# A decoder block on one core: where the small products stand among the dense ones, from the first columns to the attention

## The chip, the cores and the metric

One Trainium2 chip, one of its cores. The time is that of one execution on the device in microseconds (us). TensorE (PE in the profile) does matrix products, VectorE (DVE), ScalarE (ACT) and GpSimd (POOL) work element by element, SyncE (SP) issues most DMAs. Each engine takes its instructions in the order in which the program lists them; across engines they wait on semaphores.

## What is computed

A hybrid decoder block for 1024 tokens of 1024 channels: attention over low-rank latents (8 heads) and an RWKV-7 recurrence (8 heads of 64), merged by sigmoid gates, then a feed-forward and a gated embedding.

```python
h = rmsnorm(x, g_mix)
z_mla, z_rwkv, z_gate = split(h @ w_in)            # 672, 1792 and 2048 columns
# recurrence: token shift of z_rwkv, then r, k, v (512 columns each) and three low-rank inputs
decay = exp(-exp(-softplus(-(w0 + tanh(w_lo) @ w2)) - 0.5)); a = sigmoid(a0 + a_lo @ a2); g = sigmoid(g_lo) @ g2
kk = k * k_k / norm(k * k_k)
S_t = S_{t-1} diag(decay_t) + (S_{t-1} a_t) b_t^T + v_t k_t^T ;  y_t = S_t r_t     # 1024 steps
y_b = (groupnorm(y) + bonus) * g @ w_o_rwkv
# attention: q and k, v from normed latents, rotary tables of 32 dimensions, causal softmax
y_a = attention(rmsnorm(c_q) @ w_uq, rmsnorm(c_kv) @ w_ukv, rope(k_pe)) @ w_o_mla
x = x + (sigmoid(gate_a) * y_a + sigmoid(gate_b) * y_b) @ w_out
x = x + relu(h2 @ w_ffn_up)**2 @ w_ffn_down ;  x = x + sigmoid(h3 @ w_ple_gate) * (p @ w_ple_proj) ;  rmsnorm(x)
```

## The kernel before

The columns of `h @ w_in` are made 128 at a time by `dense`: the weights are split into a high and a low part (`wh` by ACT, `wl` by DVE), and 48 products of 128x128 by 128x512 (`psd<-xh,wh`, `psd<-xl,wh`, `psd<-xh,wl`; 8 blocks, 3 terms, 2 halves) fill one accumulator, which ACT and DVE then evacuate. 16 such units are the columns of the gates (`gate_units`); nothing reads them before the merge after the attention, so the kernel uses them as filler.

The generators yield an estimate of the work they have traced, and `weave` traces the stream that is furthest behind its share. That decides the order on each engine. The stages are:

- **First columns** (52 to 142 us): the columns of the low-rank inputs (`evac_lo`), two of the four key columns (`evac_k`; two came earlier), then 12 low-rank accumulators (`lora`: decay, a and g), the norm of the keys (`n`, `sn`, `rn`, `rns`: ACT and DVE on 8 rows), the first two r columns (`evac_rv`), and the products `nb`, which spread the norm over the channels for `kz`.
- **Early stage** (142 to 367 us): the stream `main` (columns of the latents, the rest of r, v, then gate units) is woven with `early(g)` for 8 groups of 128 tokens and with two triangular inverses. `inverse` has a long DVE part (`prd`, `X`), a way through DRAM (`xt_d`, `mt`), two transposes on DVE (`x0`), and then small products of 32x32 (`y<-x,lr` and `y<-mt,y2s`, called y products below). The second inverse is the last of the stage.
- **Recurrence** (367 to 575 us): per group `pre(g+1)` loads and prepares the next group, `chain` does two chunks of 64 tokens (products `pc`, solve, `py`, `vT`, the new state W), `finish` normalises (`yT`, `yn`, `yh`, `yl`). Gate units go between them, in half columns (`pg`). `T_LATE` and `T_MAIN` set the shares. `T_LEFT = 60` (in the scheduler's own units) is kept back.
- **Preparation** (575 to 644 us): the last `finish`, and then the attention's latents (`latf`, split into `chi` and `clo`), rotary tables (`posi`, `tab`, `kpr`), value weights, first values and queries, woven with the gates kept back (`T_REST`).
- **Attention, merge, feed-forward, embedding** (from 644 us).

`tc.issue_after(ins)` puts the instructions that are traced inside it behind `ins` on their own engine. In `together` the first product of a bundle may move up, and the rest stand behind it:

```python
first = mms[0]()
with tc.issue_after(first.ins):
    for f in mms[1:]:
        last = f()
```

Of the kernel before, what the change touches and what calls it, by code (L numbers as in the profile page):

```python
# [11 lines left out]
F32 = mybir.dt.float32  # L12
# [57 lines left out]
def tile_block(  # L70
# [147 lines left out]

    def mm_steps(acc, wh, wl, kb, rh, rl):

        for wt, rr in ((wh, (rh, rl)), (wl, (rh,))):
            for k in range(kb):
                for ri, r in enumerate(rr):
                    for h in range(2):
                        T.matmul(acc[:, h, :], lhsT=wt[:, k, :], rhs=r[k][:, h * 512:h * 512 + 512],  # L225
                                 start=wt is wh and k == 0 and ri == 0, stop=wt is wl and k == kb - 1)
                yield 0.43 * len(rr)
# [30 lines left out]
    def run(g):  # L258
        for _ in g:
            pass  # L260
# [5 lines left out]
    def lazy(f):  # L266
        yield from f()

# [86 lines left out]
    with s0:  # L355
# [91 lines left out]
        run(dense(w_in, 0, NB, MLA_COLS + RD + 2 * P, 2 * P, xh, xl, evac_k, m0=2))  # L447
# [8 lines left out]
        for which in range(3):  # L456
            for j in range(4):
                cs = slice(j * P, (j + 1) * P)
                acc = psd(s="lora")
                terms = [(wt, t) for wt in (lw_h, lw_l) for t in lora_in[which]]  # L460
                if which == 2:
                    terms.pop()
                for h in range(2):
                    hs = slice(h * 512, h * 512 + 512)
                    for i, (wt, t) in enumerate(terms):
                        T.matmul(acc[:, h, :], lhsT=wt[:, which, cs], rhs=t[:, hs], start=i == 0, stop=i == len(terms) - 1)
                t = ta("sa")
                if which < 2:
                    A.activation(t, flat(acc), AF.Sigmoid, bias=pcol(("w0", "a0")[which], j))
                    nc.sync.dma_start(sa_d[which, cs, :], t)  # L470
                else:
                    A.copy(t, flat(acc))
                    nc.sync.dma_start(g_d[cs, :], t)
# [23 lines left out]
        run(dense(w_in, 0, NB, MLA_COLS, RV0 * P, xh, xl, evac_rv))  # L497

        for j in range(4):
            acc = psd(s="nb")  # L500
            for h in range(2):
                T.matmul(acc[:, h, :], lhsT=selt[0:32 + H, j, :], rhs=rns[0:32 + H, h * 512:h * 512 + 512], start=True, stop=True)
            V.scalar_tensor_tensor(kz[j], kz[j], pcol("k_k", j), flat(acc), ALU.mult, ALU.mult)
            nc.sync.dma_start(kh_d[j * P:(j + 1) * P, :], kz[j])

    p0.close()

    with ExitStack() as wk:
# [32 lines left out]
        def norm_latent(ms, n, g, i):  # L541
            rb = te("rb")
            sumsq_rstd(src["early"], sqt[ms[0] >= 3], n, rb, i)
# [24 lines left out]
        def until(g, cost):  # L568

            done = 0.0  # L570
            while done < cost:
                c = next(g, None)
                if c is None:
                    return
                done += c
                yield c

        def latent_cols():
            q = dense(w_in, 0, NB, 0, QR, xh, xl, evac_c)
            yield from dense(w_in, 0, NB, QR, KVR, xh, xl, evac_c, m0=3)  # L580
            yield from until(q, 12)
            yield from norm_latent((3, 4), KVR, "g_kv", 0)
            yield from q
            yield from kpe_raw()
            yield from norm_latent((0, 1, 2), QR, "g_q", 1)
# [3 lines left out]
            dense(w_in, 0, NB, MLA_COLS + RV0 * P, RD - RV0 * P, xh, xl, evac_rv, m0=RV0),  # L589
# [3 lines left out]
        def gate_units():  # L593

            for m in range(2 * NB):
                raw = load_w(w_in, 0, NB, G0 + m * P, P)
                wh, wl = split_w([(lambda t: t, raw)], NB, P)
                if "half" not in psq:
                    acc = psd()
                    yield from mm_steps(acc, wh, wl, NB, xh, xl)  # L600
                    evac_gate(m, acc)
                    continue
                t = src["gt"]()
                for h in range(2):
                    hs = slice(h * 512, h * 512 + 512)
                    acc = psq["p"].tile([P, 512], F32, tag="pg", bufs=2, name=nm("pg")) if "half" in psq else psd()[:, 0, :]
                    for wt, rr in ((wh, (xh, xl)), (wl, (xh,))):
                        for k in range(NB):
                            for ri, r in enumerate(rr):
                                T.matmul(acc, lhsT=wt[:, k, :], rhs=r[k][:, hs], start=wt is wh and k == 0 and ri == 0, stop=wt is wl and k == NB - 1)  # L610
# [36 lines left out]
        with ExitStack() as rg:  # L647
            ep = src["early"] = pool(rg, "early")

            def early(g):  # L650
# [14 lines left out]
                for c in range(2):  # L665
                    ps = psa((P, 4, CH), s="L")
                    for j in range(4):
                        for h in range(2):
                            R = LOH[h]
                            T.matmul(ps[R, j, :], lhsT=c8(a)[R, 2 * j + c, :], rhs=c8(ah)[R, 2 * j + c, :], start=True, stop=True)  # L670
# [5 lines left out]
            def inverse(b):  # L676
# [31 lines left out]
                yield 3  # L708
                for c in range(8):
                    y2 = psa((P, 4, CH), s="y2")  # L710
                    for j in range(4):
                        for h in range(2):
                            Rt, Rb = slice(h * 64, h * 64 + 32), slice(h * 64 + 32, h * 64 + 64)
                            T.matmul(y2[Rb, j, 0:32], lhsT=lr[Rt, c * 4 + j, :], rhs=x0[Rt, c * 4 + j, :], start=True, stop=True)
# [22 lines left out]
        with ExitStack() as rg:  # L737
            kp = pool(rg, "late")

            def pre(g):  # L740
# [37 lines left out]
                for c in range(2):  # L778
                    ar = kp.tile([P, 8, CH], F32, tag="ar", bufs=4, name=nm("ar"))
                    scs = psx.tile([P, 2, 4, P], F32, tag="sc", bufs=1, name=nm("sc"))  # L780
                    for j in range(4):
                        for h in range(2):
                            R = LOH[h]
                            T.matmul(scs[:, h, j, :], lhsT=sh[R, 2 * j + c].rearrange("q b t -> q (b t)"),
                                     rhs=q3[R, h:3:2 - h, 2 * j + c, :], start=True, stop=True)
# [27 lines left out]
            def chain(ci):  # L813
# [37 lines left out]
                yield 1  # L851
# [19 lines left out]
                yield 1  # L871
# [52 lines left out]
    with ExitStack() as rg:  # L924
# [12 lines left out]
        def rope_tables():  # L937
# [22 lines left out]
            t, kpr = slot(12, F32, "kpt"), slot(16, F32, "kpr")  # L960
# [15 lines left out]
        with ExitStack() as pst:  # L976
# [82 lines left out]
            prep = chainit(latents(), lazy(rope_tables), value_weights(), values(0, V0, psa_v), queries(0, psv))  # L1059
# [686 lines left out]
```

## Time and profile before

| what | value |
|---|---|
| median of 3 runs | 1776.8 us (1774.46 to 1779.6) |
| profiled execution | 1779.02 us, of which 1777.3 us from its first to its last instruction |
| mean granted TensorE clock | 0.984 |
| PE busy | 1700.4 us (96% of the span) |
| DVE, ACT, POOL busy | 1199.6, 834.2 and 259.4 us |

A wait row names the engine and tile that waited, the engine and tile that ended the wait, the total, the number of times and the longest. A timeline row has the start, the length, engine, line, operation, tiles and count, and in brackets the idle time of that engine just before. The chain of waits goes back from the last instruction over what released each one.

### The profile page before, as it was taken

To read this page: it belongs to the slowest core of one execution; us is meant where nothing else is said; L and a number is where in the kernel's file an instruction comes from. 1 tells how busy PE (TensorE), PEld (TensorE's weight loads), DVE (VectorE), ACT (ScalarE), POOL (GpSimd) and SP (SyncE) were. 2 spreads that over 40 slices of the span, in tenths; PEclk is the share of its full clock that TensorE was granted. 3 is DMA by queue.
4 is the path that set the end of the run, shared out by engine and by line. 5 is a ranking of instruction groups with operands and counts; after the bars stand their busy time and mean duration, and the time that the engine had idled before them with its cause. 6 is when DMAs were issued, how large, how long until landed. Compare 5 with 4: busy or idle time off the path is not lost.

```text
span 1777.3 us, 26927 instructions
## 1 busy us (share of the span) xinstructions
PE 1700.4 (96%) x10525; PEld 1382.4 (78%) x10525; DVE 1199.6 (67%) x1882; ACT 834.2 (47%) x1418; POOL 259.4 (15%) x206
## 2 busy tenths in 40 slices
PE   7999999799999989998999999999999999999997
PEld 6877877677777867776888877888888888888886
DVE  6546695857777578887264368555568787687655
ACT  5553424244443366665344156555566344354444
POOL 2000000000000022121000203333332333332000
PEclk9999999989999999999999999999999999999999
DMA  6257765645553510015353324535557755451402
GB/s 196 72 204 217 202 199 128 183 102 140 159 141 96 168 44 25 25 60 190 107 153 108 110 116 143 166 131 159 167 182 249 238 167 160 148 178 48 154 12 96
DMA packets 245695, 246.14 MB, mean 138 GB/s; under 512 B 48729, under 2 KB 194752, under 8 KB 245568
## 3 DMA queue, kind: packets, MB, share of 16 engines
q1 hardware_dynamic: 243792, 239.65, 43.8%
q0 software_dynamic: 1760, 4.76, 0.8%
q8 instruction: 83, 1.36, 0.3%
q14 instruction: 44, 0.36, 0.1%
q10 hardware_dynamic: 16, 0.00, 0.0%
HBM read 162.31 MB, written 81.54 MB: 137 GB/s over the span
## 4 chain that ended last, share of the span: by engine, by line
PE 68%; DVE 16%; ACT 5%; DMA 5%; issue 4%; POOL 1%; SPq 1%; DVEq 0%; ACTq 0%; POOLq 0%
PE psd L225 22%; PE psX L1394 17%; PE psY L1394 8%; PE psZ L1394 4%; PE pg L610 2%; PE pb L234 2%; PE po L1147 2%; DVE prd L689 1%; PE pT L1130 1%; PE k L234 1%; DMA r<-rkv_d 1%; DVE wl L216 1%; PE qp L234 1%; DVE xb L319 1%; ACT prob L1110 1%
## 5 line engine op out<-in xcount | busy, mean ns | idle before, releaser
L1394 PE MATMUL psX<-xb,sw 128*128 128x512 f32 x768 | 177.7, 390 | 2.1 <-ACT hid L1497 1.2
L1394 PE MATMUL psX<-hb,sw 128*128 128x512 f32 x768 | 177.1, 389 | 0.4 <-DVE res L1558 0.4
L1394 PEld LDWEIGHTS psX<-xb,sw 128*128 128x128 f32 x768 | 143.9, 188 | 33.1 <-ACT hid L1497 1.6
L1394 PEld LDWEIGHTS psX<-hb,sw 128*128 128x128 f32 x768 | 144.1, 188 | 30.7 <-issue 0.8
L215 ACT CAST wh<-wr 128x1024 fp32r<-128x1024 f32 (+2 forms) x72 | 62.2, 869 | 150.6 <-PE psd L225 128.8
L319 DVE TENSOR_TENSOR sw<-sw,sw 128x512 fp32r<-128x512 f32 x128 | 93.9, 738 | 56.0 <-ACT sw L318 55.8
L318 ACT CAST sw<-sw 128x512 fp32r<-128x512 f32 x128 | 79.4, 620 | 102.1 <-PE psX L1394 36.1
L225 PE MATMUL psd<-xh,wh 128*128 128x512 f32 x384 | 122.8, 399 | 0.5 <-ACT yn L888 0.5
L225 PE MATMUL psd<-xl,wh 128*128 128x512 f32 x384 | 121.8, 396 | 0.0
L216 DVE TENSOR_TENSOR wl<-wr,wh 128x1024 fp32r<-128x1024 f32 (+2 forms) x72 | 72.6, 1009 | 48.6 <-PE psd L225 28.8
L318 ACT CAST sw<-wr 128x512 fp32r<-128x512 f32 x96 | 59.3, 622 | 71.0 <-PE psX L1394 39.1
L225 PE MATMUL psd<-xh,wl 128*128 128x512 f32 x384 | 92.0, 390 | 0.0
L1394 PE MATMUL psY<-hb,sw 128*128 128x512 f32 x384 | 89.6, 389 | 0.0
L1394 PE MATMUL psY<-xb,sw 128*128 128x512 f32 x384 | 89.6, 389 | 0.0
L319 DVE TENSOR_TENSOR sw<-wr,sw 128x512 fp32r<-128x512 f32 x96 | 80.6, 840 | 11.3 <-ACT sw L318 11.2
L319 DVE TENSOR_TENSOR hb<-braw,hb 128x1024 fp32r<-128x1024 f32 x56 | 78.6, 1403 | 10.9 <-ACT hb L318 10.8
L225 PEld LDWEIGHTS psd<-xh,wh 128*128 128x128 f32 x384 | 72.5, 191 | 16.9 <-ACT yn L888 1.0
L225 PEld LDWEIGHTS psd<-xl,wh 128*128 128x128 f32 x384 | 72.9, 190 | 15.8
L318 ACT CAST hb<-braw 128x1024 fp32r<-128x1024 f32 x56 | 58.7, 1048 | 55.1 <-DMA braw<-hid_d 23.5
L225 PEld LDWEIGHTS psd<-xh,wl 128*128 128x128 f32 x384 | 72.0, 188 | 15.4
L1394 PEld LDWEIGHTS psY<-xb,sw 128*128 128x128 f32 x384 | 72.1, 188 | 15.0
L1394 PEld LDWEIGHTS psY<-hb,sw 128*128 128x128 f32 x384 | 72.1, 188 | 15.0
(416 smaller groups left out, 3753.3 us busy)
## 6 DMA issues: line engine op xcount, KB each, us to landing
hid_d<-hid SPq DMA_DIRECT2D x112, 256.0 KB, 4.3
braw<-hid_d SPq DMA_DIRECT2D x56, 512.0 KB, 4.4
wr<-in_w_in_dram SPq DMA_DIRECT2D x35, 512.0 KB, 5.3
wr<-in_w_ffn_up_dram SPq DMA_DIRECT2D x32, 512.0 KB, 5.1
wr<-in_w_ffn_down_dram SPq DMA_DIRECT2D x32, 512.0 KB, 4.1
gate_d<-gt SPq DMA_DIRECT2D x16, 512.0 KB, 3.2
gate<-gate_d SPq DMA_DIRECT2D x16, 512.0 KB, 3.7
xt<-in_x_dram SPq DMA_DIRECT2D x8, 512.0 KB, 8.6
```

Source lines behind the costliest of these rows:

```text
L215: A.copy(dst(wh), src)
L216: V.tensor_tensor(dst(wl), src, dst(wh).bitcast(F32), ALU.subtract)
L225: T.matmul(acc[:, h, :], lhsT=wt[:, k, :], rhs=r[k][:, h * 512:h * 512 + 512], start=wt is wh and k == 0 and ri == 0, stop=wt is wl and k ...
L234: T.matmul(acc, lhsT=wt[:, k, :], rhs=r[k][:, sl], start=wt is wh and k == 0 and ri == 0, stop=wt is wl and k == kb - 1)
L318: A.copy(hi, src)
L319: V.tensor_tensor(lo, src, hi.bitcast(F32), ALU.subtract)
L610: T.matmul(acc, lhsT=wt[:, k, :], rhs=r[k][:, hs], start=wt is wh and k == 0 and ri == 0, stop=wt is wl and k == NB - 1)
L689: V.tensor_tensor(pv, X[:, 0:t, 0:t], U[:, 0:t, t].unsqueeze(1).to_broadcast([P, t, t]), ALU.mult)
L1110: A.activation(pr_t[:, :n].rearrange("q (a b) -> q a b", a=pieces), sc[:, :pieces, :w], AF.Exp, bias=nmx, accum_out=rs)
L1130: T.transpose(out=tp_[:, b * P:(b + 1) * P], in_=prs[i][:, (4 * g + b) * P:(4 * g + b + 1) * P], identity=ident)
L1147: return T.matmul(po[i * 64:i * 64 + 64, 0:P], lhsT=vt[kb // 2][:, kb % 2, h * 64:h * 64 + 64], rhs=pts[i][:, kb * P:(kb + 1) * P], start= ...
L1394: T.matmul(acc, lhsT=w[:, wl_, j, :], rhs=part(b, xl_, j), start=start and s == 0, stop=key == LAST[bank] and s == len(steps) - 1, skip_gr ...
```

## The change

1. Every dense product is remembered (`dense_last`). `together` puts the first product of a bundle behind the last dense product that has been traced; it is now used for the `L` products, for the first y products of the inverse and for the `sc` products too. The transposes of the latents' norms stand behind the last dense product as well, and the norm is split in two (`latent_rstd`, `norm_latent`) with a share of columns between.
2. The low-rank products are woven with the last two key columns; the `nb` products are traced among the last steps of the first r columns.
3. The inverse yields 16 in place of 3 ahead of its y products; the chain yields 2 in place of 1 ahead of its state products, and no longer yields at its end.
4. In the preparation the rotary tables are traced ahead of the latents, which get five slots of their own instead of two; the helper tile `kpt` moves from slot 12 to 23.

```diff
+    dense_last = [None]
+    def behind_dense():
+        return tc.issue_after(dense_last[0])
...
+        run(weave([(dense(w_in, 0, NB, MLA_COLS + RD + 2 * P, 2 * P, xh, xl, evac_k, m0=2), 20.6), (low_rank(), 24)]))
...
-        run(dense(w_in, 0, NB, MLA_COLS, RV0 * P, xh, xl, evac_rv))
+        first_r = dense(w_in, 0, NB, MLA_COLS, RV0 * P, xh, xl, evac_rv)
+        run(until(first_r, 18))
         for j in range(4):
+            run(until(first_r, 1))
             acc = psd(s="nb")
...
+        run(first_r)
...
             yield from dense(w_in, 0, NB, QR, KVR, xh, xl, evac_c, m0=3)
-            yield from until(q, 12)
-            yield from norm_latent((3, 4), KVR, "g_kv", 0)
+            yield from until(q, 8)
+            r = latent_rstd((3, 4), KVR)
+            yield from until(q, 8)
+            yield from norm_latent(r, (3, 4), "g_kv", 0)
             yield from q
             yield from kpe_raw()
-            yield from norm_latent((0, 1, 2), QR, "g_q", 1)
+            r = latent_rstd((0, 1, 2), QR)
+            rest_r = dense(w_in, 0, NB, MLA_COLS + RV0 * P, RD - RV0 * P, xh, xl, evac_rv, m0=RV0)
+            yield from until(rest_r, 8)
+            yield from norm_latent(r, (0, 1, 2), "g_q", 1)
+            yield from rest_r
...
         def together(*mms):
-            first = mms[0]()
+            with behind_dense():
+                first = mms[0]()
             with tc.issue_after(first.ins):
                 for f in mms[1:]:
-                    last = f()
-            return last
+                    f()
...
-                yield 3
+                yield 16
                 for c in range(8):
                     y2 = psa((P, 4, CH), s="y2")
...
                 if next_mms:
                     put_values(Wn)
-                yield 1
+                yield 2
...
                 V.tensor_reduce(ys[:, c * 4:c * 4 + 4], sq, AX.X, ALU.add)
-                yield 1
...
-            t, kpr = slot(12, F32, "kpt"), slot(16, F32, "kpr")
+            t, kpr = slot(23, F32, "kpt"), slot(16, F32, "kpr")
...
-                    t = slot((12, 13)[n % 2], F32, "latf")
+                    t = slot((12, 13, 19, 20, 24)[n], F32, "latf")
...
-            prep = chainit(latents(), lazy(rope_tables), value_weights(), values(0, V0, psa_v), queries(0, psv))
+            prep = chainit(lazy(rope_tables), latents(), value_weights(), values(0, V0, psa_v), queries(0, psv))
```

**The order on PE at the second inverse.** Before, the y products follow the last dense product of the early stage (a gate unit, `psd_2924`) without anything between them; `x2` counts products of one row:

```order
L225 MATMUL psd_2924<-xh_171,wl_2921 128x512 x2
L225 MATMUL psd_2924<-xh_172,wl_2921 128x512 x2
L714 MATMUL y_351_2803<-x_348_2774,lr_2775 32x32
L714 MATMUL y_353_2833<-x_348_2774,lr_2775 32x32
L714 MATMUL y_351_2803<-x_348_2774,lr_2775 32x32 x7
L714 MATMUL y_353_2833<-x_348_2774,lr_2775 32x32 x7
L722 MATMUL y_351_2803<-mt_1198,y2s_2812 32x32 x8
L722 MATMUL y_353_2833<-mt_1198,y2s_2842 32x32 x8
L714 MATMUL y_355_2859<-x_348_2774,lr_2775 32x32 x8
```

After, the same y products (`y_371` and on) lie among the products of two gate units:

```order
L735 MATMUL y_371_3027<-x_353_2872,lr_2873 32x32 x8
L231 MATMUL psd_3010<-xh_169,wh_3006 128x512 x2
L231 MATMUL psd_3010<-xl_177,wh_3006 128x512
L744 MATMUL y_371_3027<-mt_1198,y2s_3036 32x32 x8
L231 MATMUL psd_3010<-xl_177,wh_3006 128x512
L735 MATMUL y_373_3053<-x_353_2872,lr_2873 32x32 x8
L231 MATMUL psd_3010<-xh_170,wh_3006 128x512 x2
L231 MATMUL psd_3010<-xl_178,wh_3006 128x512
L744 MATMUL y_373_3053<-mt_1198,y2s_3062 32x32 x8
L231 MATMUL psd_3010<-xl_178,wh_3006 128x512
```

Gate units ahead of the recurrence's first product (`vT` of its first chunk) are 4 before and 8 after. Before, ten gate products of a ninth half column (`pg`) stand between the last y product and `vT`; after, none.

**The order on PE where the recurrence ends.** `yT` is the transposition of the last group's `finish`. Before, it is followed by the rest of a gate unit and by three whole ones (48 products each) ahead of the attention's products:

```order
L610 MATMUL pg_5677<-xh_168,wl_5647 128x512
L881 MATMUL yT_5638<-ident,yc_5406 64x64 x16
L610 MATMUL pg_5677<-xh_169,wl_5647 128x512
L610 MATMUL pg_5677<-xh_170,wl_5647 128x512
L610 MATMUL pg_5677<-xh_171,wl_5647 128x512
L610 MATMUL pg_5677<-xh_172,wl_5647 128x512
L225 MATMUL psd_5770<-xh_165,wh_5766 128x512 x2
L225 MATMUL psd_5770<-xl_173,wh_5766 128x512 x2
```

After, the last gate products stand ahead of `yT`, and the attention's first values (`v`) follow it:

```order
L634 MATMUL pg_5793<-xh_170,wl_5594 128x512
L634 MATMUL pg_5793<-xh_171,wl_5594 128x512
L634 MATMUL pg_5793<-xh_172,wl_5594 128x512
L900 MATMUL yT_5863<-ident,yc_5630 64x64 x16
L1033 MATMUL v_5988<-wvh_5982,chi_5920 128x512
L1033 MATMUL v_6088<-wvh_5982,chi_5920 128x512
L1033 MATMUL v_5988<-wvh_5982,clo_5921 128x512
L1033 MATMUL v_5988<-wvl_5983,chi_5920 128x512
```

Between the first `vT` and the recurrence's last state products lie 367 `pg` before and 370 after; 14 more follow ahead of `yT` after, 51 before. The three whole units behind `yT` and the rest have gone ahead of the recurrence.

**The order of the DMAs on SP at the preparation.** Before, the transfers of `latf` are issued behind the last store of the recurrence (`yb_d<-yl`), with `posi` third, and other loads between; `kpr` is the last but one:

```order
L896 DMA yb_d<-yl_5724 128x4x128
L989 DMA latf_5755<-lat_d 128x1024
L989 DMA latf_5787<-lat_d 128x1024
L943 DMA posi_5889<-in_positions_dram 128x1024
L115 DMA wr_6397<-in_w_ukv_dram 128x2x256
L1038 DMA uq_6576<-in_w_uq_dram 128x3x192
L989 DMA latf_5809<-lat_d 128x1024
L522 DMA gate_d<-gt_5827 128x1024
L989 DMA latf_5841<-lat_d 128x1024
L961 DMA kpr_5948<-kpr_d 64x1024
```

After, `posi` goes first and two `latf` follow; `kpr` has the tile of `posi` (slot 16), so its transfer waits for DVE's conversion of `posi`, and three `latf` are queued behind it:

```order
L914 DMA yb_d<-yh_5901 128x4x128
L915 DMA yb_d<-yl_5902 128x4x128
L962 DMA posi_5934<-in_positions_dram 128x1024
L1008 DMA latf_5958<-lat_d 128x1024
L1008 DMA latf_5962<-lat_d 128x1024
L980 DMA kpr_5953<-kpr_d 64x1024
L1008 DMA latf_5966<-lat_d 128x1024
L1008 DMA latf_5970<-lat_d 128x1024
L1008 DMA latf_5974<-lat_d 128x1024
```

## Rows read from the trace of the kernel before

**Rows 1.** Busy time by stretch, all engines; the last three columns are clock, DMA, GB/s.

```profile
142.00:345.00 203.00, 198.26 (x1299) 160.09 (x1298) 150.74 (x227) 70.21 (x113) 3.93 (x4) 0.98 0.67 189
345.00:367.00 22.00, 10.09 (x257) 8.62 (x258) 6.45 (x10) 11.53 (x37) 0.00 (x0) 0.58 0.82 188
367.00:575.00 208.00, 195.00 (x2519) 153.58 (x2520) 154.96 (x353) 87.08 (x176) 0.00 (x0) 0.98 0.46 128
575.00:644.00 69.00, 65.67 (x319) 52.72 (x314) 44.60 (x65) 30.86 (x52) 7.26 (x8) 1.00 0.44 136
```

**Rows 2.** Timeline of PE around the second inverse.

```profile
340.74 0.62 PE L225 MATMUL psd<-xl,wh 128*128 128x512 f32 x2
341.20 3.79 PE L225 MATMUL psd<-xh,wl 128*128 128x512 f32 x16
353.83 0.42 PE L714 MATMUL y<-x,lr 32*32 32x32 f32 x4 [8.85 <-DVE x L707]
...
366.68 0.80 PE L610 MATMUL pg<-xh,wh 128*128 128x512 f32 x1 [0.62 <-ACT mt L725]
...
371.25 1.12 PE L805 MATMUL vT<-ident,v 64*64 64x64 f32 x16
```

**Rows 3.** Timeline of PE at the first inverse's y products, first and last row.

```profile
286.52 0.69 PE L714 MATMUL y<-x,lr 32*32 32x32 f32 x28
...
296.64 0.74 PE L225 MATMUL psd<-xh,wh 128*128 128x512 f32 x2
```

**Rows 4.** Waits of PE from 50 to 366 us.

```profile
PE rT L293 <- DVE rr L207: 2.0, 1, 2.0
PE nb L502 <- DVE zs L387: 1.4, 1, 1.4
PE lora L466 <- ACT sa L469: 1.3, 2, 1.0
PE lora L466 <- DVE kz L387: 0.7, 1, 0.7
```

**Rows 5.** Timeline of DVE at the end of the keys' norm.

```profile
135.87 1.22 DVE L488 TENSOR_TENSOR rns<-rn,rns 8x1024 fp32r<-8x1024 f32 x1 [1.87 <-ACT rns L487]
```

**Rows 6.** Waits of PE from 366 to 575 us.

```profile
PE pc L852 <- ACT W L848: 5.7, 5, 1.9
PE pc L833 <- DVE W L859: 4.2, 3, 1.6
```

**Rows 7.** The chain of waits over one group: start, length, what.

```profile
488.34 1.15 PE yT L881 x32
...
494.76 0.70 DVE yl L319
...
497.78 5.56 DMA r<-rkv_d
503.43 0.70 DVE q L764
...
515.74 1.15 PE yT L881 x32
```

**Rows 8.** The chain of waits after the recurrence's last state products.

```profile
575.25 11.81 PE pg L610 x51
587.05 1.08 PE yT L881 x32
588.13 1.14 PE pg L610 x4
...
593.86 5.36 DMA latf<-lat_d
```

**Rows 9.** Timeline of DVE from 575 to 646 us.

```profile
580.26 0.69 DVE L879 TENSOR_TENSOR yc<-yc,rr 128x512 f32<-128x512 f32 x1
...
592.66 0.69 DVE L319 TENSOR_TENSOR yl<-yn,yh 128x512 fp32r<-128x512 f32 x1 [0.74 <-ACT yh L318]
...
603.86 0.69 DVE L944 CAST tab<-posi 128x1024 f32<-128x1024 int32 x1
...
622.79 0.76 DVE L958 TENSOR_SCALAR tab<-tab,freq_sb 128x1024 f32<-128x1024 f32 x1 [2.45 <-ACT tab L957]
...
641.80 0.69 DVE L319 TENSOR_TENSOR kl<-kn,kh 64x512 fp32r<-64x512 f32 x1 [0.83 <-ACT kh L318]
```

**Rows 10.** Timeline of PE at the attention's first score.

```profile
644.06 0.28 PE L1100 MATMUL s<-kh,q 96*128 96x256 f32 x1
```

More of the change, by code (lines that the diff above doesn't have):

```diff
@@ L267, in lazy, with until @@
         yield from f()
+    def until(g, cost):
+        done = 0.0
+        while done < cost:
+            c = next(g, None)
+            if c is None:
+                return
+            done += c
+            yield c
     def weave(streams, lead=False):
@@ L455, in tile_block, with low_rank @@
         split_act(lraw, lw_h, lw_l)
[L456 to L473, printed above, removed]
+        def low_rank():
+            for which in range(3):
+                for j in range(4):
+                    cs = slice(j * P, (j + 1) * P)
+                    acc = psd(s="lora")
+                    terms = [(wt, t) for wt in (lw_h, lw_l) for t in lora_in[which]]
+                    if which == 2:
+                        terms.pop()
+                    for h in range(2):
+                        hs = slice(h * 512, h * 512 + 512)
+                        for i, (wt, t) in enumerate(terms):
+                            T.matmul(acc[:, h, :], lhsT=wt[:, which, cs], rhs=t[:, hs], start=i == 0, stop=i == len(terms) - 1)
+                    t = ta("sa")
+                    if which < 2:
+                        A.activation(t, flat(acc), AF.Sigmoid, bias=pcol(("w0", "a0")[which], j))
+                        nc.sync.dma_start(sa_d[which, cs, :], t)
+                    else:
+                        A.copy(t, flat(acc))
+                        nc.sync.dma_start(g_d[cs, :], t)
+                    yield 1.7
+        run(weave([(dense(w_in, 0, NB, MLA_COLS + RD + 2 * P, 2 * P, xh, xl, evac_k, m0=2), 20.6), (low_rank(), 24)]))
         n2, sn, rn = (ta(n)[:H] for n in ("n2", "sn", "rn"))
@@ L609, in gate_units @@
                             for ri, r in enumerate(rr):
[L610 removed]
+                                mm = T.matmul(acc, lhsT=wt[:, k, :], rhs=r[k][:, hs], start=wt is wh and k == 0 and ri == 0, stop=wt is wl and k == NB - 1)
+                            dense_last[0] = mm.ins
                             yield 0.215 * len(rr)
@@ L666, in early @@
                     ps = psa((P, 4, CH), s="L")
[L667 to L670, printed above, removed]
+                    together(*[lambda j=j, R=R: T.matmul(ps[R, j, :], lhsT=c8(a)[R, 2 * j + c, :], rhs=c8(ah)[R, 2 * j + c, :], start=True, stop=True)
+                               for j in range(4) for R in LOH])
                     lt = ep.tile([P, 4, CH], F32, tag="lt", bufs=3, name=nm("lt"))
@@ L780, in pre @@
                     scs = psx.tile([P, 2, 4, P], F32, tag="sc", bufs=1, name=nm("sc"))
[L781 to L785, printed above, removed]
+                    together(*[lambda j=j, h=h: T.matmul(scs[:, h, j, :], lhsT=sh[LOH[h], 2 * j + c].rearrange("q b t -> q (b t)"),
+                                                         rhs=q3[LOH[h], h:3:2 - h, 2 * j + c, :], start=True, stop=True)
+                               for j in range(4) for h in range(2)])
                     for h in range(2):
```

31 lines of the change are left out of this document (13 added, 18 removed).

## The prediction

> **What bounds the kernel now.** I read the busy time by stretch first, then PE's timeline and waits at the places that the order moves, then the chain of waits. PE holds the time nearly everywhere: it is busy for 198.3 of the 203 us of the early stage, for 195.0 of 208 in the recurrence and for 65.7 of 69 in the preparation [rows 1]. Nothing is removed from PE's work: the 16 gate units stay, at about 11.0 us each (two products take 0.46 us from one start to the next, 340.74 to 341.20, so 48 take 11.0) [rows 2]. So the change can only win what PE loses to waiting and to a low clock, and it has to leave as little waiting elsewhere.
>
> Before the attention three places offer something. First, the hole at the second inverse: the last gate unit ends at 341.20 + 3.79 = 344.99, the y products wait 8.85 us for DVE's transposition `x`, then run one after another, and the recurrence's first product starts at 366.68: 21.7 us [rows 2], at 0.58 of the clock on the mean [rows 1]. Second, the recurrence: 13.0 us idle over 208, mostly before `pc` [rows 1, 6]. Third, the preparation: it lasts from 575.25, when the last state and output products end, to 644.06, the first score, 68.8 us [rows 8, 10]. It looks dense, but only because gate products fill it: 51 + 4 `pg` and three units.
>
> **The first columns.** The low-rank products wait 1.3 + 0.7 us for their evacuations [rows 4]; with key columns between them that should go, -2.0. But the casts that make `rns` now stand behind the evacuation of the second r column on ACT and on DVE, where they stood ahead of it. Before, only the third `nb` product waits for that evacuation, 1.4 us [rows 4]; after, all do, and the cast of 1.22 us, which itself waited 1.87 us for ACT's, comes on top [rows 5]: between 1.2 and 3.1 us more. I take 2.0 for it, and the part comes to 0, from -2 to +3.
>
> **The early stage.** Four more gate units ahead of the recurrence: +44.0. The hole of 21.7 us goes, since the y products lie between dense ones. They still take PE's time. The first inverse's already lie so: from 286.52 to 296.64 are 10.1 us with eleven single dense products of 0.23 us between, so 7.6 us are theirs [rows 3]; +7.6. The second `rT` has a wait of 2.0 us now [rows 4] and stands behind 38 dense products after; -2.0. The `L` products stay where they were. Sum: 44.0 - 21.7 + 7.6 - 2.0 = **+27.9**. The hole is filled twice over: 22 us would have done.
>
> **The recurrence.** The dense share is nearly the same (367 and 370 `pg`), so little is taken from PE; only ten `pg` and `vT` at half clock at its head are gone from it, whose excess I count below. The period between two `yT` is 27.4 us (488.34 to 515.74), and the chain of waits runs through it without PE's dense products being most of it: `yT`, `yn`, `yl` at 494.76, SP's queue, 5.56 us of loading `r`, then DVE's rows from 503.43 for the next group up to the next state products [rows 7]. The loads of the next group stand behind `yl`'s store on SP in both orders. `bo` follows `yT` directly after the change, which puts DVE's `bv` ahead of W in most groups: that keeps DVE as long. The gaps before `pc` (5.7 + 4.2 us [rows 6]) are filled by products that stand in front of them, but the loop behind them is not shorter. I take 0; it could lie between -13.0 (all idle time of the stage gone) and +5 (0.7 us for each of seven groups, one more DVE instruction ahead of W, by the 0.70 of a 512-wide one [rows 7]).
>
> **The preparation.** No gate product is left to cover it, so its length is that of its chain. From the last output products: 5.7 us to the normalised `yc` (575.25 to 580.95), now waited for by `yT` at once instead of at 587.05; 1.2 for `yT`; 5.2 from its end at 588.13 to `yl` at 593.35; 0.5 for the stores on SP's queue; then `posi` goes first, and I give it 5.4, since a `latf` takes 5.36 [rows 8, 9]. From there DVE works through tables, low parts and queries: 603.86 to 642.49 are 38.6 us now [rows 9]. Two low parts that stood ahead come in (+2.4, at 1.2 each), the splits of the query weights go out, and two query instructions fill the 2.45 us in which DVE waits for the sine: I take 37. `kpr` waits for the conversion of `posi`, and three `latf` are queued behind it, so they land some 6 us after `posi`; DVE has 9 us of tables and low parts until it needs the third. From DVE's last low part to the first score 1.6 us (642.49 to 644.06) [rows 9, 10]. Sum: 5.7 + 1.2 + 5.2 + 0.5 + 5.4 + 37 + 1.6 = 56.6 in place of 68.8: **-12.2**, between -18 and -6.
>
> So 33 us of gate products go out of the preparation and only 12 come back. That is the point of the forecast: there the filler was in the right place, under a DVE chain.
>
> **The clock.** At 366.68 to 371.25 PE, after the y products, runs ten `pg` and goes on at about half pace: 0.457 us a product in place of 0.23, 2.3 us lost [rows 2], and the stretch before shows 0.58 of the clock, so about the lower of the two levels, 1.2 of 2.4 GHz [rows 1]. This restart goes away, and one comes at the values and queries behind an idle PE in the preparation, where the clock is 1.00 now [rows 1]: -2.3 and +2.3.
>
> The Trainium skill, "TensorE: Matmul & The Clock Gate", section "HAM oscillation — how this bites in real kernels", says that a product stage which is shorter than the wait ahead of it starts at the slow clock again each time. The trace agrees at the one wait of 8.85 us; by that rule the uncovered preparation would run most of its products slowly, which is the second rival below and speaks against this change.
>
> **Sum.** 0 + 27.9 + 0 - 12.2 + 0 = +15.7. The profiled execution took 1779.02, 2.2 above the median of 1776.8; 1779.0 + 15.7 = 1794.7, and against the median **1792**.
>
> **The rivals.**
> 1. *Faster: the tables are ready before the recurrence ends.* If `posi` doesn't wait for the last `yT`, the rotary tables run under the last group. The way to `posi` (5.2 + 0.5 + 5.4 = 11.1) and the tables (DVE's 603.86 to 622.79 + 0.76 without low parts and weights, some 15) come off the chain: 15.7 - 26.1 = -10.4, 1766. It decides from 21 us taken off. Against it: on SP `posi` stands behind the last `yb_d<-yl`, which needs `yT`, and DVE's conversion behind `yl`. For it: nothing but that a tile's place could come free sooner than I read. 0.13.
> 2. *Slower still: half clock through the preparation.* The products ahead of the first score (78, of 0.23 us) are 18 us at full pace, and 36 at half. Part of this lies under DVE's chain; if half of it shows, +9: 1801. For it: PE would wait there in stretches longer than the 8.85 us that preceded the slow stretch [rows 2]. Against it: DVE, not PE, sets the chain. 0.12.
> 3. *Same: the recurrence becomes bound by PE.* With a share of dense products ahead of each bundle, the gaps of 13.0 us close [rows 1]: 15.7 - 13.0 = +2.7, 1779.5. For it: the gaps before `pc` are short, at most 1.9 us [rows 6], and 4 to 10 products stand ahead now. Against it: the loop through SP and the load of `r` is as long as the period [rows 7]. 0.16.
> 4. *The change doesn't do what it says* in the first columns: the weave gives its 2 us, `nb` takes them back. That is within the sum; with the gates where they were it would be a change of nothing, but the order shows them moved. 0.03 for a time that stays.
>
> **How the numbers follow.** This kernel's runs spread by 0.3% (1774.46 to 1779.6), so I call 5.3 us the least that a measurement can tell. The likeliest case, 0.56, is +15.7 with its own bounds: first columns -2 to +3, preparation -6 to +6 around its value, recurrence up to +5, so 1783 to 1803. Almost all of it is slower (0.51), a little the same (0.05). Rival 2 adds 0.12 to slower, rival 3 gives 0.12 the same and 0.02 on either side, rival 1 0.13 faster. Slower 0.65, same 0.20 (0.05 + 0.12 + 0.03), faster 0.15. The range takes in rival 3 and rival 2 and leaves rival 1 out: 1774 to 1804.
>
> **What would show it.** Right: `yT` of the last group some 28 us later than now (587.05 less the wait behind the gate products, so about 609), the y products spread over two gate units and no idle time of several us before the recurrence, periods of the recurrence near 27.4 us, and a preparation of 50 to 62 us in which PE waits for DVE and for loads. Wrong: a preparation below 45 us (rival 1), recurrence periods near 25.5 us with `pc` never waiting (rival 3), or a second inverse whose y products wait again in front of the dense ones.

## The result and the profile after

The changed kernel takes 1791.71 us (median of 7 runs, 1787.48 to 1798.39), the kernel before beside it 1778.0 (7 runs, 1774.46 to 1780.52): a ratio of 1.0089 (95% interval 1.0074 to 1.0104), 13 to 18 us slower (15.8 by the ratio, 13.7 between the two medians). The profiled execution took 1797.95 us, near the upper end of its runs and at a mean clock of 0.979, with a span of 1796.2. That is 18.9 us over the span before; the shares below add up to it.

Busy time of the changed kernel by stretch (early stage, recurrence, preparation), then the same cuts for the kernel before, since [rows 1] were cut at round times; columns as in [rows 1]:

```profile
146.72:398.83 252.11, 250.10 (x1747) 198.74 (x1746) 162.18 (x242) 90.29 (x159) 3.80 (x4) 0.99 0.65 179
398.83:605.72 206.89, 193.09 (x2516) 152.32 (x2515) 151.40 (x351) 86.18 (x175) 0.00 (x0) 0.98 0.45 126
605.72:662.09 56.37, 29.66 (x125) 21.85 (x125) 40.08 (x59) 24.54 (x43) 7.42 (x8) 0.70 0.39 114
```

```profile
142.36:366.68 224.32, 207.68 (x1555) 168.32 (x1554) 156.72 (x234) 81.42 (x149) 3.93 (x4) 0.94 0.69 188
366.68:575.25 208.57, 195.56 (x2522) 154.08 (x2522) 155.32 (x353) 87.41 (x177) 0.00 (x0) 0.98 0.46 127
575.25:644.06 68.81, 65.48 (x309) 52.57 (x310) 44.35 (x65) 30.85 (x51) 7.26 (x8) 1.00 0.44 136
```

The first cut is the end of the `nb` products. So all that lies ahead of it is 4.4 us longer (142.36 to 146.72), the early stage 27.8, the recurrence 1.7 shorter, the preparation 12.4 shorter, and the untouched rest 0.9 longer. In the early stage PE is now busy for 250.1 of 252.1 us: hardly anything is idle there, and yet it is the stage that loses. In the preparation PE is busy for 29.7 of 56.4 us, at 0.70 of the clock.

Of the 4.4 us, 3.2 are lost before the first columns begin: their first dense product starts at 55.40 in place of 52.16. The split of the low-rank weights (`lw_l`) is now traced ahead of the last key columns, and on DVE it gets in front of two `xl`, for which PE waits. Timeline of DVE before (first two rows) and after, then PE's wait after:

```profile
30.07 0.87 DVE L322 SCALAR_TENSOR_TENSOR xl<-xT,pc_mix,xh 128x256 fp32r<-128x256 f32 x2
31.39 1.76 DVE L319 TENSOR_TENSOR lw_l<-lraw,lw_h 128x1536 fp32r<-128x1536 f32 x1 [0.46 <-ACT lw_h L318]
...
30.17 1.75 DVE L336 TENSOR_TENSOR lw_l<-lraw,lw_h 128x1536 fp32r<-128x1536 f32 x1
31.83 0.87 DVE L339 SCALAR_TENSOR_TENSOR xl<-xT,pc_mix,xh 128x256 fp32r<-128x256 f32 x2
...
32.36 0.45 PE L241 MATMUL k<-xl,wh 128*128 128x256 f32 x1 [1.44 <-DVE xl L339]
```

This wait of 1.44 us is in every profile of the changed kernel and its variants, and not in the kernel before or in e1. That the split's new place makes it is read from the two orders; no run moves the split alone. The other 1.7 us are a stretch at a lower clock behind it (0.72 from 30 to 36 us), which e10 has too and e2, e3 and e5 have not; these start the first columns at 53.6 to 53.7.

Timeline of PE in the changed kernel, where [rows 2] show the wait of 8.85 us: the second inverse's y products, first and last rows, and the recurrence's start.

```profile
371.31 0.44 PE L735 MATMUL y<-x,lr 32*32 32x32 f32 x16
372.26 0.39 PE L231 MATMUL psd<-xl,wh 128*128 128x512 f32 x1
372.58 0.44 PE L744 MATMUL y<-mt,y2s 32*32 32x32 f32 x16
...
391.65 0.44 PE L744 MATMUL y<-mt,y2s 32*32 32x32 f32 x16
392.02 0.50 PE L231 MATMUL psd<-xl,wh 128*128 128x512 f32 x1
...
398.83 0.68 PE L825 MATMUL vT<-ident,v 64*64 64x64 f32 x16
```

No row has a wait: the hole is gone. The recurrence's first `vT` comes 27.6 us later than at 371.25 [rows 2]; the cut used above for the kernel before, 366.68, lies ahead of the ten gate products at half clock that precede it there.

Waits of PE in the changed kernel, in three stretches (first columns; recurrence; preparation); they answer to [rows 4] and [rows 6]:

```profile
PE nb L524 <- DVE rns L508: 4.5, 1, 4.5
...
PE pc L853 <- DVE W L879: 7.3, 5, 2.3
PE yT L900 <- DVE yc L898: 3.7, 6, 0.9
PE pc L861 <- DVE qs L856: 1.9, 1, 1.9
...
PE v L1033 <- ACT chi L335: 12.7, 1, 12.7
PE kn L241 <- DVE t L1071: 11.5, 2, 10.4
PE yT L900 <- DVE yc L898: 1.7, 1, 1.7
```

The waits for `lora` and `rT` are gone, as was read from the order. In their place `nb` waits 4.5 us at once. The recurrence waits as much as before, at other products. The preparation has two waits of over 10 us.

Timeline of DVE in the changed kernel: the norm of the keys, then the preparation (the latter answers to [rows 9]).

```profile
123.18 0.68 DVE L499 TENSOR_SCALAR n<-n 8x1024 f32<-8x1024 f32 x1 [1.58 <-ACT n L498]
...
139.68 0.67 DVE L506 TENSOR_SCALAR rn<-rn 8x1024 f32<-8x1024 f32 x1
140.28 1.26 DVE L404 SCALAR_TENSOR_TENSOR zs<-psd,pc_rest,zs 128x1023 f32<-128x1023 f32 x1
141.58 1.22 DVE L508 TENSOR_TENSOR rns<-rn,rns 8x1024 fp32r<-8x1024 f32 x1
...
610.09 0.69 DVE L898 TENSOR_TENSOR yc<-yc,rr 128x512 f32<-128x512 f32 x1
615.78 0.69 DVE L336 TENSOR_TENSOR yl<-yn,yh 128x512 fp32r<-128x512 f32 x1 [0.74 <-ACT yh L335]
621.90 0.69 DVE L963 CAST tab<-posi 128x1024 f32<-128x1024 int32 x1 [4.23 <-issue]
...
658.79 0.69 DVE L336 TENSOR_TENSOR kl<-kn,kh 64x512 fp32r<-64x512 f32 x1 [0.32 <-ACT kh L335]
```

The preparation can be set beside the prediction's own steps: 605.72 to 610.78 to the normalised `yc` (5.1 us, 5.7 forecast), `yl` done at 616.47, `posi` converted from 621.90 (5.4, 5.9 forecast), DVE's work from there to 659.48 (37.6, 37 forecast), and then 2.6 us to the first score at 662.09 (1.6 forecast). The chain of waits shows what the last step is:

```profile
653.59 2.90 PE kn L241 x6
656.49 4.93 PE v L1033 x20
661.45 0.59 ACT vt L1035
662.09 0.39 PE s L1119
```

Twenty value products stand between the last `kn` products, which wait for DVE, and the first score. The score itself waits for `vt`, the evacuation of these value products, and no longer for DVE.

### The profile page after: what moved, and what is told of

Read it like the earlier page. It is cut to its first block, busy times and chain, and to the rows that moved or that the text cites. A ratio compares the mean times of both kernels' runs of the same rounds, so it can differ in the third digit from the quotient of the medians.

```text
span 1796.2 us, 26888 instructions
## 1 busy us (share of the span) xinstructions
PE 1706.1 (95%) x10525; PEld 1382.4 (77%) x10525; DVE 1197.9 (67%) x1882; ACT 835.3 (47%) x1417; POOL 260.1 (14%) x206
## 4 chain that ended last, share of the span: by engine, by line
PE 71%; DVE 17%; ACT 4%; DMA 4%; issue 3%; POOL 1%; SPq 1%; DVEq 0%; POOLq 0%; ACTq 0%
PE psd L231 24%; PE psX L1413 17%; PE psY L1413 8%; PE psZ L1413 4%; DMA r<-rkv_d 2%; PE pb L241 2%; PE pg L634 2%; PE po L1166 2%; PE pT L1149 1%; PE k L241 1%; DVE wl L216 1%; PE qp L241 1%; DVE prd L712 1%; DVE xb L336 1%; PE s L1119 1%
## 5 line engine op out<-in xcount | busy, mean ns | idle before, releaser
L1413 PEld LDWEIGHTS psX<-hb,sw 128*128 128x128 f32 x768 | 144.1, 188 | 31.6 <-ACT sw L335 1.8
L231 PE MATMUL psd<-xh,wh 128*128 128x512 f32 x400 | 128.0, 399 | 0.3 <-DVE zs L404 0.3
L231 PE MATMUL psd<-xl,wh 128*128 128x512 f32 x400 | 127.8, 397 | 0.0
L1072 POOL TENSOR_TENSOR t<-t,t 32x512 f32<-32x512 f32 x16 | 20.5, 1281 | 618.7 <-DVE t L1071 573.4
L231 PE MATMUL psd<-xh,wl 128*128 128x512 f32 x400 | 99.0, 394 | 0.0
```

The costliest lines, as they stand in the source:

```text
L231: mm = T.matmul(acc[:, h, :], lhsT=wt[:, k, :], rhs=r[k][:, h * 512:h * 512 + 512], start=wt is wh and k == 0 and ri == 0, stop=wt is wl a ...
L1072: G.tensor_tensor(t1[R], t1[R], t2[R], ALU.add)
L1413: T.matmul(acc, lhsT=w[:, wl_, j, :], rhs=part(b, xl_, j), start=start and s == 0, stop=key == LAST[bank] and s == len(steps) - 1, skip_gr ...
```

## The experiments

Each was timed in five rounds against the kernel before on its chip; a difference in us is the ratio's, taken on the median before (1774 to 1778).

**One number alone (e1).** The kernel before with

```diff
-                yield 3
+                yield 16
                 for c in range(8):
```

> The kernel before with one number of the change: the inverse yields 16 in place of 3 ahead of its y products. Eight gate units then stand ahead of the recurrence and none is left for the preparation. Theory (the loss is where the filler stands): early stage +28 us, preparation -12 us, recurrence within 3 us, so 13 to 17 us above the kernel before, as the whole change. Rival (the loss comes from the other parts: the keys' norm, the order of the tables, the bundles behind dense products): within 5 us of the kernel before.

Measured: 1.0065 (1.0046 to 1.0083), +11.5 us. The stretches of its profile:

```profile
141.94:397.86 255.92, 252.26 (x1746) 200.13 (x1746) 163.39 (x243) 90.19 (x159) 3.94 (x4) 0.98 0.64 179
397.86:599.06 201.20, 188.30 (x2515) 149.01 (x2514) 153.26 (x351) 85.20 (x175) 0.00 (x0) 1.00 0.47 130
599.06:651.54 52.48, 27.75 (x125) 21.00 (x126) 38.03 (x55) 22.78 (x38) 6.34 (x7) 0.73 0.36 114
```

The early stage pays 31.6 us and the preparation gives back 16.3: the theory's pattern, with the sum 1.5 us below the range that was given. The recurrence is 7.4 us shorter than before, which was not expected. The ten half-clock products ahead of `vT` (366.68 to 371.25) are 4.6 of it; counted from `vT`, 204.0 us become 201.2, at a clock of 1.00.

**All but the number (e2).** The changed kernel with

```diff
-                yield 16
+                yield 3
                 for c in range(8):
```

> The changed kernel with the inverse's yield put back to 3: four gate units ahead of the recurrence, three left for the preparation, all other parts of the change kept. Theory: the hole of some 22 us at the second inverse is back, the preparation is long again (65 to 69 us), the first columns keep their 4 us; 1 to 6 us above the kernel before. Rival (the other parts make the loss): 10 to 14 us above it.

Measured: 0.9977 (0.9962 to 0.9991), -4.1 us: faster than the kernel before, outside both expectations. Its stretches:

```profile
145.02:364.11 219.09, 206.43 (x1556) 167.29 (x1555) 155.79 (x234) 80.84 (x146) 3.79 (x4) 0.94 0.70 191
364.11:570.63 206.52, 195.93 (x2526) 153.78 (x2522) 153.21 (x353) 88.47 (x179) 0.00 (x0) 0.98 0.46 129
570.63:636.53 65.90, 65.03 (x310) 52.72 (x310) 44.02 (x65) 30.95 (x51) 7.42 (x8) 1.00 0.43 140
```

What lies ahead of the early stage loses 2.7 us (1.5 of it by the `xl` wait), the early stage gains 5.2 with the hole still in it (its y products wait 8.64 us), the recurrence gains 2.1 and the preparation 2.9. So with the yield at 3 the rest of the change is a gain of about 4 us, and the one number turns it into a loss: some 20 us (15.8 + 4.1) hang on it here, 11.5 in the kernel before (e1). The parts do not simply add. With the yield at 16 the rest of the change adds 4.3 us (15.8 - 11.5) instead of taking 4.1 off; the intervals of e1 and of the changed kernel overlap, so that cost is not settled; e5 shows where some 3 us of it would lie.

**Keys first (e3).** The changed kernel with

```diff
-        run(weave([(dense(w_in, 0, NB, MLA_COLS + RD + 2 * P, 2 * P, xh, xl, evac_k, m0=2), 20.6), (low_rank(), 24)]))
+        run(dense(w_in, 0, NB, MLA_COLS + RD + 2 * P, 2 * P, xh, xl, evac_k, m0=2))
+        run(low_rank())
```

> The changed kernel with the low-rank products put back behind the last two key columns. Theory: the norm of the keys starts 5 us earlier, the 4.5 us wait of the nb products goes, and part of the half clock behind it; 4 to 7 us faster than the changed kernel. Rival (the wait comes from the casts standing behind the evacuation, by the place of the nb products, not by the keys' end): no gain, within 2 us of the changed kernel, since the nb products keep their place in the text.

Measured: 1.0074 (1.0057 to 1.0091), +13.1 against the changed kernel's +15.8. That is less than the 4 to 7 that were expected, and the two intervals overlap, so the 2.7 us are not settled by the times. The profile shows where they would come from. The norm starts at 119.17 instead of 123.18, and `nb` no longer waits for it:

```profile
119.17 0.68 DVE L500 TENSOR_SCALAR n<-n 8x1024 f32<-8x1024 f32 x1 [11.77 <-ACT n L499]
```

```profile
PE lora L483 <- ACT sa L486: 1.3, 2, 1.0
PE nb L525 <- DVE kz L526: 0.8, 2, 0.5
PE lora L483 <- DVE kz L404: 0.7, 1, 0.7
```

`nb` ends at 142.70 in place of 146.72. Of these 4.0 us, 1.8 had been lost before the first columns (they start at 53.61 here and at 55.40 in the changed kernel's profile); 2.2 are the keys'. The `nb` products stand where the changed kernel has them in the text, and still they don't wait for `rns`: the rival's mechanism falls.

**Six units ahead instead of eight (e4).** As e2, with `yield 8`.

> The changed kernel with the inverse's yield at 8: six gate units ahead of the recurrence instead of eight, one and a half left for the preparation. Theory: two units are what the hole takes, the early stage is 22 us shorter than in the changed kernel, and the preparation takes the gate products under its DVE chain for 0 to 8 us: 14 to 20 us faster than the changed kernel, so 0 to 6 us faster than the kernel before. Rival (gate products cost their full time in the preparation too): within 6 us of the changed kernel.

Measured: 1.0014 (0.9999 to 1.0028), +2.5 us, so 13 us faster than the changed kernel and just outside what was expected. Two steps of the expectation fail. The early stage, up to the first `vT`, is 14.8 us shorter than in the changed kernel (237.3 and 252.1), not 22: the first y products now stand ahead of a gate unit, and PE waits again.

```profile
PE y L735 <- DVE x L730: 6.4, 1, 6.4
```

And the preparation takes 66.7 us, though PE has 12 us less work there than in e2 (52.9 and 65.0). Chain of waits of e4 from its last output products:

```profile
576.08 0.47 PE py L874 x16
576.55 11.58 PE pg L634 x50
588.13 1.08 PE yT L900 x32
```

The gate products stand ahead of `yT`, whose input is ready 5 to 6 us after `py`; all that follows starts 6 us late. The kernel before has the same block, 11.81 us [rows 8]; there the preparation is full of PE's work anyway.

**Latents first (e5).** The changed kernel with

```diff
-            t, kpr = slot(23, F32, "kpt"), slot(16, F32, "kpr")
+            t, kpr = slot(12, F32, "kpt"), slot(16, F32, "kpr")
...
-                    t = slot((12, 13, 19, 20, 24)[n], F32, "latf")
+                    t = slot((12, 13)[n % 2], F32, "latf")
...
-            prep = chainit(lazy(rope_tables), latents(), value_weights(), values(0, V0, psa_v), queries(0, psv))
+            prep = chainit(latents(), lazy(rope_tables), value_weights(), values(0, V0, psa_v), queries(0, psv))
```

> The changed kernel with the preparation's order as before: two latents, then the positions, the latents in two slots, kpt in slot 12. Theory (the uncovered preparation is a chain through the positions, the tables on DVE and kpr): the positions land 1 to 2 us later and the third to fifth latent wait for slots: the preparation is 1 to 5 us longer than in the changed kernel (56.4). Rival (kpr's wait for DVE's conversion, with three latents queued behind it, makes the new order worse): 2 to 5 us shorter than in the changed kernel.

Measured: 1.0077 (1.0057 to 1.0098), +13.7. Against the changed kernel's +15.8 that is within the intervals. The profile has the preparation at 53.3 us (597.90 to 651.23) instead of 56.4, the rival's side. e3, with the tables first, has 55.5, so the difference holds. In this kernel `posi` is converted 3.1 us later after the last output products (617.20 - 597.90 = 19.3, against 16.2), as the theory said, and the first `kn` product starts 2.9 us later (45.1 and 42.2). It ends earlier all the same: from there to the first score it takes 8.3 us in place of 14.2, since no value product stands behind the `kn` products:

```profile
642.95 0.77 PE L241 MATMUL kn<-chi,wh 128*128 128x512 f32 x1 [9.96 <-DVE t L1071]
...
651.23 0.33 PE L1119 MATMUL s<-kh,q 96*128 96x256 f32 x1
```

The value products are all done by 633, ahead of this wait. What the rival named, `kpr` behind the conversion, was not tested by itself.

**Less ahead of yT, the preparation full (e6), and e8, e9: the same with room in it.** All three cut the block ahead of the last `yT`:

```diff
-            run(until(main, 10))
+            run(until(main, 5))
```

e6 has the yield at 3. e8 has it at 8 and e9 at 6, both with the keys first (the diff of e3).

> The changed kernel with the inverse's yield at 3 (as in e2), and half as many gate products ahead of the last group's transposition yT (21 in place of 51; the others stay, behind it). Theory A (with three and a half units left the preparation is full of PE's work): within 3 us of e2, since PE has 65 us of products there either way. Theory B (the chain from yT sets the end, and the 51 products ahead of it delay it by 6 us): 5 to 7 us faster than e2.

> As e4 (yield 8: six gate units ahead of the recurrence), with 17 gate products in place of 51 ahead of the last yT, and with the low-rank products behind the last key columns. Theory: the two units and a half that are left, 30 us, now lie under the chain from yT to the first score instead of ahead of it, so the preparation is 56 to 60 us in place of 66.7; with 3 to 4 us from the keys' norm, 9 to 14 us faster than e4, so 7 to 12 us faster than the kernel before. Rival (gate products cost their time wherever they stand in the preparation): within 5 us of e4.

> As e8, with the yield at 6: five gate units ahead of the recurrence and one more unit left for the preparation. Theory: the hole at the second inverse is half filled (one unit less ahead of it, 11 us idle back in part), the preparation is full (64 to 67 us): 0 to 6 us slower than e8. Rival (the unit costs the same at either place): within 2 us of e8.

Measured: e6 0.9987 (0.9972 to 1.0001), -2.3 us, as e2 within the intervals: theory A holds. `yT` comes 5 us sooner, and the preparation is 66.9 us long, full of products. e8 0.9973 (0.996 to 0.9985), -4.8 us: 7.3 faster than e4, short of the 9 to 14 that were expected. The edit left 27 gate products ahead of `yT`, not 17. Its preparation against e4's (second row):

```profile
575.69:636.43 60.74, 53.33 (x240) 41.99 (x241) 41.85 (x63) 27.92 (x48) 7.94 (x8) 0.92 0.40 129
```

```profile
576.55:643.26 66.71, 52.85 (x240) 40.50 (x241) 42.22 (x63) 28.30 (x49) 7.43 (x8) 0.92 0.38 118
```

The same products, 6.0 us less: that is the time by which `yT` came sooner (6.4 us after `py` instead of 11.6), and a bit over. e9 0.9964 (0.9949 to 0.998), -6.4 us, not slower than e8 as the theory had it; the 1.6 us between them are within the intervals, as the rival had it. Its preparation is 59.0 us with 28 products more in it, at a clock of 1.00, and not the 64 to 67 that were expected.

**More work than the changed kernel (e10).** Two gate units are computed twice, and the block ahead of `yT` is cut as in e6:

```diff
-            for m in range(2 * NB):
+            for m in [*range(2 * NB), 0, 1]:
...
-        spent = [16 * 10.3]
+        spent = [18 * 10.3]
```

> The changed kernel with two gate units computed a second time (units 0 and 1, at the end of the gate stream, the same result written twice): 96 products more than the changed kernel does in all, 82 of them behind the last yT, where the preparation has none in the changed kernel. PE's work grows by 22 us. Theory (the uncovered preparation is a chain through DVE and loads under which 20 us of dense products are free, and they hold the clock up): within 4 us of the changed kernel. Rival (the preparation is bound by PE, or dense products get in the way there): 12 to 22 us slower than the changed kernel.

Measured: 1.0119 (1.0105 to 1.0134), against the changed kernel's 1.0089 (1.0074 to 1.0104): 5.3 us slower, for 22 us more work. Its preparation:

```profile
599.11:661.38 62.27, 49.57 (x220) 37.53 (x221) 42.11 (x63) 27.78 (x48) 7.45 (x8) 0.89 0.40 124
```

PE is busy for 19.9 us more there than in the changed kernel, and the stretch is 5.9 us longer. So about 14 of 20 us are free, what the higher clock gives back included; 1.4 of the 5.9 are `yT`, later again. It is neither quite the theory (within 4) nor the rival (12 to 22), but far nearer to the theory.

**Latents first where filler covers (e11); the low-rank products woven with r columns (e12).** e11 is e9 with the diff of e5. e12 is e9 with

```diff
         run(dense(w_in, 0, NB, MLA_COLS + RD + 2 * P, 2 * P, xh, xl, evac_k, m0=2))
-        run(low_rank())
...
-        run(until(first_r, 18))
+        run(weave([(until(first_r, 18), 18), (low_rank(), 16)]))
```

> e9 with the preparation's order as before (two latents, then the positions; two slots). Theory (tables first pays only where gate products cover the end of the preparation, since the attention's products then don't have to run last and slowly): 0 to 4 us slower than e9. Rival (latents first is better everywhere, as e5 against the changed kernel): 2 to 4 us faster than e9.

> e9 with the low-rank products woven with the first r columns instead of standing between the keys and these: the keys still come first, so the norm's chain has the same products to hide under. Theory: the 2 us in which the low-rank products wait for their evacuations go, and nb waits no longer than 2 us: 0 to 3 us faster than e9. Rival (the evacuations of the low-rank products now stand on ACT between the norm's steps): nb waits over 3 us, 1 to 4 us slower than e9.

Measured: e11 0.9994 (0.9981 to 1.0007), 5.3 us slower than e9, more than was expected, and its preparation is 62.0 us instead of 59.0. Tables first pays where gate products cover the chain; 3.0 of the 5.3 us are seen in the preparation, and the rest was not traced. e12 0.9958 (0.9943 to 0.9973), -7.4 us: the fastest of all by its median, 1766.56, and within the interval of e9, so that the gain of 0 to 3 us can't be told from none. `lora` waits 0.2 us in place of 2.0, `nb` 1.4.

## Why the prediction was right

**What decides.** The forecast was +15.7, from +27.9 in the early stage and -12.2 in the preparation; the profile shows +27.8 and -12.4. The step that carried it was to count gate units ahead of the recurrence in the order, at 11.0 us each, against the hole of 21.7, and not to take "PE no longer waits" for a gain. e1 shows the same pattern by itself, and e2 that the rest of the change makes no loss where the filler stays in the preparation.

That the sum meets the ratio to 0.1 us is luck. The profiled execution is 18.9 us longer, not 15.8, and the terms miss in both directions: +4.4 ahead of the early stage where 0 was forecast, and -12.4 in the preparation where the restart that was booked apart (+2.3) makes the forecast -9.9.

**The early stage.** The y products went between dense ones, the waits for `x` and `rT` went, and four units came. e1, with none of the new bundles, has the same number of gate units ahead and 255.9 us, against 251.4 to 252.6 in four profiles with the new order (the changed kernel, e3, e5, e10). So the bundles and the split norms are worth some 4 us there, of which 1.8 is the wait for `rT` that e1 still has; the rest was not traced. The prediction had 2.

**The recurrence.** Forecast 0, with the half-clock start booked apart at -2.3; measured -1.7. This is one profile: e3 and e5, with the same products in the stage, take 201.4 us for it at a clock of 1.00 where the changed kernel's profile takes 206.9 at 0.98. So the term is not known to better than 5 us. One part of it is missing in the prediction: of the ten products that left the head of the stage it took off the excess of 2.3 us, but not the 2.3 us that they take at full clock. Periods between `yT` at 463.23, 491.39, 517.02 and 546.17 are 28.2, 25.6 and 29.1 us, around the 27.4 of [rows 7]. The gaps moved from state products to others and did not close: rival 3 is out for this kernel. e1 and e3, with the old and the new bundles, have 201.2 and 201.4 us for the stage: the new order in the recurrence did nothing that can be seen.

**The preparation.** It was forecast at 56.6 us and took 56.4, and no step was off by more than 1.0 us; the last `yT` starts at 610.83 (about 609 forecast). Rival 1 is out: `posi` is converted 16.2 us after the last output products, behind the last stores. But the last step is not the one that was written down. The first score does not wait for DVE's last low part, done at 659.48; it waits for the value products and their evacuation. e5 shows the difference: `posi` later by 3.1 us, and the score sooner by as much. The way through the tables sets the time up to the `kn` products, and what PE has in its order behind them sets the rest. That a cover is free there for the most part is shown by e10: 14 of 20 us.

**What lies ahead of the early stage: the step that failed.** The prediction took 0 (from -2 to +3) for the first columns and left out all that comes before them; the profile shows +4.4. Counted from their first dense product, the first columns last 91.3 us in place of 90.2, within the bounds. The other 3.2 us are the wait for `xl` and the low clock behind it: moving the low-rank products between the key columns also moved the split of their weights, and the prediction followed the products alone. Inside the first columns the sizes offset, and one of them has another cause. The casts of `rns` do stand behind an evacuation, by 1.3 us (140.28 to 141.58). But the wait of `nb` is 4.5 us because the norm itself starts late: weaving the low-rank products with the keys moves the keys' end back, so that `n` begins 67.8 us after the first dense product (123.18 - 55.40), 65.6 in e3 and 65.5 in the kernel before. The chain from `n` to `rns` takes 19.6 us (123.18 to 142.80), 19.4 in e3, and only two r columns are left to cover it. The prediction looked at the queue in front of the last link and not at where the chain begins.

**The clock.** Half of rival 2 came true: the clock in the preparation is 0.70. The time shows little of it, since PE waits there anyway. On the chain lie the last six `kn` products and the first two value products behind them: the six take 2.7 us from the first of them to the product behind them (653.59 to 656.29), and in e10 the same six take 1.5 (654.39 to 655.85). With the two, that is about 1.6 us, an estimate from these rows, where 2.3 were booked. The prediction weighed a rule of the Trainium skill ("TensorE: Matmul & The Clock Gate", section "HAM oscillation — how this bites in real kernels"): a stage of products shorter than the wait ahead of it starts slowly each time. The trace agrees in the clock: behind the wait of 10.4 us the `kn` products start 0.43 us apart, and late value products 0.23. e10, at 0.89 of the clock, does not separate the clock from the work, since it has 96 products more.

**The better kernel.** e9 and e12 beat both: the gate units are divided so that the hole is partly filled (in e9 the first y products still wait 6.7 us), the preparation keeps 158 gate products, and the block ahead of `yT`, 28 products or 6.5 us, is hardly longer than the 5 to 6 us that its input takes.

## What to carry to other kernels

Filler is worth what the hole it fills is long, and costs its full time beyond it: count the units that the order puts ahead of a dependent stage, and compare with the wait in us, before you call a wait that disappears a gain. It fills the hole only if it stands ahead of the instruction that waits: in e4 two units more left a wait of 6.4 us. Take filler first from stages that are bound by the engine it runs on, and leave it under chains of other engines. There, put it behind the instruction that starts the chain: 50 products in front of one transposition cost 6 us here, and behind it most of such products' time was free (14 of 20 us in e10). And when work is woven into a stage, look at which long chain begins at the stage's end: it begins later. Look also at what is traced with that work, on the other engines: here 1.75 us of DVE's work (`lw_l`) got in front of operands that PE needed, over 20 us before the stage began.

## What had not been expected

The untouched rest of the kernel (the same instructions, from the first score on) took 1128.48 us in one profile and 1134.63 in another:

```profile
652.20:1780.68 1128.48, 1100.92 (x5511) 902.69 (x5511) 764.99 (x1105) 559.84 (x942) 238.79 (x164) 1.00 0.40 130
```

```profile
651.23:1785.86 1134.63, 1106.85 (x5512) 907.28 (x5510) 765.26 (x1110) 560.61 (x946) 240.97 (x166) 0.99 0.40 129
```

These are e3 and e5. The rows differ in the granted clock (1.00 and 0.99) and in PE's busy time by the same 6 us, so two profiles of one kernel can differ by that much without any cause in the change. Stretches do not escape it: the recurrence took 206.9 us in the changed kernel's profile and 201.4 in these two. So differences of 2 or 3 us between experiments are left open, and of a long stretch differences of 5. What makes the clock fall in one execution and not in the other was not tried.
